# Turning the scan's output in whole 128x128 tiles, and summing log decays as two f16 products, in a hybrid attention and gated DeltaNet block

## The chip, the cores and the metric

One NeuronCore of one Trainium2 chip runs the whole kernel. The metric is device time of one execution in microseconds, the median of several runs. The five engines have queues of their own: PE (TensorE, matrix products; PEld is its weight load), DVE (VectorE), ACT (ScalarE), POOL (GpSimd) and SP (SyncE, here only an issuer of DMAs). They meet at semaphores.

## The reference, cut to what matters

A decoder block of width 1024 on 1024 tokens. One projection feeds two token mixers on the same normalised input: A, dilated sliding-window attention; B, gated DeltaNet (8 heads, key and value width 64, chunks of 64 tokens). Each is gated, projected up, and both are merged and projected out. The change touches two places of mixer B: the sums of log decays, and the way from the scan's output to the gated product.

```python
G = jnp.cumsum(gc, axis=-1)                       # log decays of a chunk
decay_incl = jnp.exp(jnp.where(causal, G[..., :, None] - G[..., None, :], -jnp.inf))
a = jnp.einsum('bhnid,bhnjd->bhnij', k_beta, kc) * decay_strict
t_inv = lax.linalg.triangular_solve(eye + a, ...)
...
o_b = _gated_delta_rule(gq, gk, gv, g, beta)
o_b = _rmsnorm(o_b, gdn_norm_w[layer]).reshape(b, s, GDN_V_WIDTH)
y_b = (o_b * jax.nn.silu(gdn_z)) @ w_up_b[layer]
```

## The kernel before

**Filler.** The big projections run as filler: `feed.tick(n)` puts n steps into PE's order, each of three f16 products of 512 columns (lines 183, 184, 185: high by high, low by high, high by low; every f32 operand of a projection is split into an f16 high part and an f16 rest). Small stages put ticks between their own steps, so that PE has work while other engines do theirs. PE's order is the order of the program, written out by hand; the order of the other engines is decided by a scheduler.

**Memory of PE's results.** PSUM is used through rings of banks of 128x512 f32, named by what they serve: mm (three buffers, the projections), G and S (two each), O (one).

**Log decays** (`in_chunks`, `decay`, lines 1110 to 1189). `gg` holds the log decays, 128 tokens (two chunks) by 8 tiles by 8 heads. Tile t holds, for the four heads of one half `hb`, a product `gm` of the decays with the triangle `upto64` on DVE, 128x256. PE multiplies `gm` by the constant triangle `later` (line 1185, f32), which gives sums of decays between every two tokens; a second product (line 1186, bf16) adds the mask; ACT takes the exponential into `E`. Two ticks follow. There are 16 such steps, 8 in each half. `gm` has two buffers, and the first two steps use a spare tile `room`, which the trace calls x.

**Triangular solve and merge** (lines 1295 to 1373). For each half `hb`, DVE inverts the 32x32 blocks in one long chain (`stmp` and `X` in turn; `As` is its input), SP writes the result out and loads it back in another layout as `T1p` and `MT`, and PE merges the blocks (`left`, line 1339, and `right`, line 1354), with DVE's `Y` between the two.

**Turning the scan's output** (lines 1731 to 1758). `ob` holds the scan's output, tokens on the partitions. Each of four channel tiles `ct` and two token halves `hf` is turned: eight f32 transposes of 64 rows (line 1745), four into a bank G and four into a bank S; DVE multiplies each bank, 256 columns, into the gate `zs[ct]` (named `zb` in the trace; two operations); ACT writes the f16 high part and DVE the f16 rest into `osb`; then two ticks. `zb`, `osb` and the low half of an output weight, `wo6l`, share a ring of five buffers, `oTb`. The eight products `ob<-ob,fac` on DVE stand just ahead, with 12 ticks behind them.

Of the kernel before, what the change touches and what calls it, by code (L numbers as in the profile page):

```python
# [10 lines left out]
F32 = mybir.dt.float32  # L11
F16 = mybir.dt.float16
BF16 = mybir.dt.bfloat16
AF = mybir.ActivationFunctionType
ALU = mybir.AluOpType
# [3 lines left out]
S = 1024  # L19
D = 1024  # L20
KT = 8
EPS = 1e-6
H_SCALE = 16.0
# [54 lines left out]
def hybrid_block(ctx: ExitStack, tc: tile.TileContext, A):  # L78
    nc = tc.nc
    V, SC, PE, GP = nc.vector, nc.scalar, nc.tensor, nc.gpsimd  # L80

    def STT(out, in0, scalar, in1, op0, op1, eng=None):
        (eng or V).scalar_tensor_tensor(out, in0, scalar, in1, op0=op0, op1=op1)  # L83

    def TT(out, in0, in1, op, eng=None):
        (eng or V).tensor_tensor(out, in0, in1, op)  # L86

    ctx.enter_context(tc.manual_schedule(engines={nc.tensor.engine}))
    base = ctx.enter_context(tc.tile_pool(name="base", bufs=1))
# [6 lines left out]
    start = [ctx.enter_context(ExitStack()) for _ in range(2)]  # L96
# [27 lines left out]
    ident = part(128)  # L124
    normw = part(KT)
    later = part(128)
# [3 lines left out]
    upto64 = part(64)  # L130
# [4 lines left out]
    gnw = part(1)  # L135
# [251 lines left out]
    feed = Feed()  # L387
# [9 lines left out]
    diag = base.tile([128, 2, 128], F32, name="diag", tag="diag", bufs=1)  # L397
# [84 lines left out]
    src = [A["w"][att_unit(2, 0, i)] for i in range(2)]  # L482
# [13 lines left out]
    with tc.manual_schedule(engines={nc.vector.engine, nc.scalar.engine}):  # L496
        wq, wk = w_first
        q, k = qk
# [63 lines left out]
        q = [bank("mm", 3), bank("O", 1)]  # L562
# [342 lines left out]

    wba = wst.tile([128, 4, 256], F32, name="wba", tag="wstage", bufs=2)[:, 0, :128].rearrange("p (k c) -> p k c", c=16)
    nc.gpsimd.dma_start(out=wba, in_=A["w_ba"])
    wbas = base.tile([128, KT, 32], F16, name="wbas", tag="diag", bufs=1)
    SC.activation(wbas[:, :, 0:16], wba, AF.Copy, scale=W_SCALE)
    STT(wbas[:, :, 16:32], wba, W_SCALE, wbas[:, :, 0:16], ALU.mult, ALU.subtract)  # L910

# [155 lines left out]
    for t in range(8):  # L1067
        tk = slice(t * 128, t * 128 + 128)
        for k in range(KT):
            PE.matmul(pba[:, t * 32:t * 32 + 32], lhsT=h_hi[:, k, tk], rhs=wbas[:, k], start=(t == 0 and k == 0),  # L1070
                      stop=False, skip_group_check=True)
            PE.matmul(pba[:, t * 32:t * 32 + 16], lhsT=h_lo[:, k, tk], rhs=wbas[:, k, 0:16], start=False,
                      stop=(k == KT - 1), skip_group_check=True)
# [5 lines left out]
    beta, gg = bg[:, 0], bg[:, 1]  # L1079
# [34 lines left out]
    def in_chunks(pg):  # L1114
        ggf = gg.rearrange("p t h -> p (t h)")
        PE.matmul(pg[:, 0:64], lhsT=upto, rhs=ggf, start=False, stop=True, skip_group_check=True)
        PE.matmul(pg[:, 64:128], lhsT=later, rhs=ggf, start=False, stop=True, skip_group_check=True)
        SC.activation(eG.rearrange("p t h -> p (t h)"), pg[:, 0:64], AF.Exp)
        by_chunk(eGs, eG)
        SC.activation(eGl.rearrange("p t h -> p (t h)"), pg[:, 64:128], AF.Exp)  # L1120
        SC.activation(dec.rearrange("p t c q -> p (t c q)"), pg[:, 128:192], AF.Exp)

    feed.later(PG_LAG, over_chunks)
    feed.tick(ATT_LEAD)
# [9 lines left out]
    p2_ = pctx.enter_context(tc.tile_pool(name="gpre2", bufs=1))  # L1134

    def bc(x, n):
        return x[..., None].to_broadcast(list(x.shape) + [n])
# [29 lines left out]
    def heads_h2(x):  # L1167
        return x.rearrange("p t (q e) -> p t e q", e=2)

    def decay(hb):  # L1170

        gh = heads_h2(gg[:, :, 4 * hb:4 * hb + 4])
        for t in range(8):
            if hb == 0 and t < 2:

                if t == 0:
                    room = wst.tile([128, 512], F32, name="x7", tag="x7", bufs=1)
                gm = room[:, 256 * t:256 * t + 256].rearrange("p (e q i) -> p e q i", e=2, q=2)
            else:
                gm = p2_.tile([128, 2, 2, 64], F32, name="gm", tag="gm", bufs=2)  # L1180
            TT(gm, bc(gh[:, t], 64), upto64[:, None, None, :].to_broadcast([128, 2, 2, 64]), ALU.mult)
            if t == 0:
                feed.tick(GM_LAG)
            p = bank("G", 2)
            PE.matmul(p[:, :256], lhsT=later, rhs=gm.rearrange("p a b c -> p (a b c)"), start=True, stop=False)
            PE.matmul(p[:, :256], lhsT=ident_b, rhs=hide_b[:, None, :].to_broadcast([128, 4, 64]),
                      start=False, stop=True)
            SC.activation(E[hb][:, t].rearrange("p a b c -> p (a b c)"), p[:, :256], AF.Exp)
            feed.tick(2)
# [269 lines left out]
    osp = {}  # L1459
    zs = {}  # L1460
    late = []
# [29 lines left out]

    def z_keep(br, ct, hf, p, rest):
        if ct not in zs:
            zs[ct] = late[1].tile([128, S], F32, name=f"zb{ct}", tag="oTb", bufs=5)
        z_silu(zs[ct][:, hf * 512:hf * 512 + 512], p, rest)

    for u in range(2):
# [159 lines left out]
    def rows(b):  # L1657
        return slice(64 * b, 64 * b + 64)
# [75 lines left out]
    for t in range(8):  # L1734
        TT(ob[:, t], ob[:, t], bc(fac[:, t], 64), ALU.mult)
    feed.tick(OB_LAG)
    for ct in range(4):
        for hf in range(2):
            ts = slice(hf * 512, hf * 512 + 512)
            ps2 = [bank("G", 2), bank("S", 2)]  # L1740
            hb, h0 = ct // 2, ct % 2 * 2
            for t in range(4):
                for b in range(2):
                    c2 = b ^ hb
                    PE.transpose(ps2[b][:, 64 * t:64 * t + 64],
                                 ob[rows(b), 4 * hf + t, 4 * c2 + h0:4 * c2 + h0 + 2].rearrange("p h v -> p (h v)"),
                                 ident[rows(b), rows(b)])
            zv = zs[ct][:, ts].rearrange("p (t c i) -> p t c i", c=2, i=64)
            for b in range(2):
                zc = zv[:, :, b ^ hb]  # L1750
                STT(zc, ps2[b][:, :256].rearrange("p (t i) -> p t i", i=64), gnw, zc, ALU.mult, ALU.mult)
            if ("b", ct) not in osp:
                osp["b", ct] = fpb.tile([128, 2, S], F16, name=f"osb{ct}", tag="oTb", bufs=5)
            n = osp["b", ct]
            sc = H_SCALE
            SC.activation(n[:, 0, ts], zs[ct][:, ts], AF.Copy, scale=sc)
            STT(n[:, 1, ts], zs[ct][:, ts], sc, n[:, 0, ts], ALU.mult, ALU.subtract)
            feed.tick(2)
    feed.until(("gate", 6))
    feed.tick(1)  # L1760
    cctx.close()
# [12 lines left out]
    for n in range(7):  # L1774
        wo7[n] = []
        for i, l in enumerate("hl"):
            if n == 5:
                t = [late[0].tile([128, 512], F32, name=f"wo5{l}{b}", tag=("gst", "oa")[i], bufs=2).bitcast(F16)
                     .rearrange("p (k n) -> p k n", n=512) for b in range(2)]
                wo7[n].append(lambda k, t=t: t[k // 2][:, k % 2])  # L1780
                continue
            if (n, l) == (6, "l"):
                t = late[1].tile([128, 2, S], F16, name="wo6l", tag="oTb", bufs=5)
                t = t.rearrange("p a b -> p (a b)").rearrange("p (k n) -> p k n", n=512)
            else:
                t = fp2.tile([128, 4, 512], F16, name=f"wo{n}{l}")
            wo7[n].append(lambda k, t=t: t[:, k])
# [2 lines left out]
    feed.flush()  # L1790

    m7.append([late[1].tile([128, 2, S], F16, name=f"mb{n}", tag=f"osa{n}" if n < 4 else "oTb",
                            bufs=1 if n < 4 else 5).rearrange("p l (k i) -> p l k i", i=256) for n in range(7)])
    fw = fp2.tile([128, D], F32, name="fw")
    nc.sync.dma_start(out=fw, in_=A["fnw"])

# [193 lines left out]
```

## Time and profile before

| | |
|---|---|
| runs of the kernel before | 1077.85, 1081.21, 1081.53 us; median 1081.21 |
| profiled execution, own time | 1077.67 us |
| its span | 1075.9 us |
| granted TensorE clock, mean | 0.998 |
| sums of log decays | 561.7 to 606.0 us (first gm to last product) |
| solve of the second half on DVE | 673.7 to 713.3 us |
| turning of the output | 889.3 to 904.4 us |

Times of the trace count from the start of the span. A row of the timeline gives start, length, engine, line, operation, what it writes and reads, the shape and a count; in brackets stands the idle time before it and who ended it. A matmul's length includes its way through the array, and the next starts before it ends, so PE's pace is the distance between starts. A row of a tile or line view gives minimum, median and maximum in ns.

### The profile page before, as it was taken

To read this page: it belongs to the slowest core of one execution; us is meant where nothing else is said; L and a number is where in the kernel's file an instruction comes from. 1 tells how busy PE (TensorE), PEld (TensorE's weight loads), DVE (VectorE), ACT (ScalarE), POOL (GpSimd) and SP (SyncE) were. 2 spreads that over 40 slices of the span, in tenths; PEclk is the share of its full clock that TensorE was granted. 3 is DMA by queue.
4 is the path that set the end of the run, shared out by engine and by line. 5 is a ranking of instruction groups with operands and counts; after the bars stand their busy time and mean duration, and the time that the engine had idled before them with its cause. 6 is when DMAs were issued, how large, how long until landed. Compare 5 with 4: busy or idle time off the path is not lost.

```text
span 1075.9 us, 23729 instructions
## 1 busy us (share of the span) xinstructions
PE 1051.3 (98%) x9430; PEld 639.9 (59%) x9430; DVE 860.6 (80%) x1977; ACT 560.1 (52%) x1272; POOL 56.9 (5%) x107
## 2 busy tenths in 40 slices
PE   7999999999999999999999999999999999999997
PEld 5995685775956855765645555555555554444443
DVE  6987997869878779979955897976588778899934
ACT  6455766566566666557634624244444345333622
POOL 0000000000000000000000001111100000000000
PEclk9999999999999999999999999999999999999999
DMA  8144531633625432741234357785685523753232
GB/s 277 62 130 106 139 104 55 168 100 88 179 70 150 110 105 63 176 114 46 75 123 162 88 130 195 244 249 164 193 268 163 160 82 121 271 195 121 78 117 79
DMA packets 99488, 148.47 MB, mean 138 GB/s; under 512 B 31136, under 2 KB 64416, under 8 KB 98224
## 3 DMA queue, kind: packets, MB, share of 16 engines
q1 hardware_dynamic: 68976, 84.60, 27.2%
q0 software_dynamic: 12320, 44.11, 13.6%
q10 hardware_dynamic: 18080, 18.23, 5.0%
q8 instruction: 74, 1.21, 0.5%
q14 instruction: 38, 0.31, 0.1%
HBM read 91.13 MB, written 36.90 MB: 119 GB/s over the span
## 4 chain that ended last, share of the span: by engine, by line
PE 68%; DVE 21%; ACT 5%; issue 2%; DMA 2%; SPq 1%; ACTq 0%; DVEq 0%
PE ps_mm L183 17%; PE ps_mm L185 16%; PE ps_mm L184 16%; DVE ca L83 3%; DVE wlo L83 2%; DVE sm L799 2%; PE ps_S L183 2%; PE ps_S L185 2%; PE ps_S L184 2%; PE ps_G L813 1%; DVE tl L86 1%; DVE rt L86 1%; SPq L629 1%; ACT sm L803 1%; PE ps_G L185 1%
## 5 line engine op out<-in xcount | busy, mean ns | idle before, releaser
L185 PE MATMUL ps_mm<-h_hi,wlo 128*128 128x512 f16 (+1 forms) x552 | 207.5, 376 | 0.0
L183 PE MATMUL ps_mm<-h_hi,whi 128*128 128x512 f16 (+1 forms) x492 | 185.0, 376 | 0.3 <-issue 0.3
L184 PE MATMUL ps_mm<-h_lo,whi 128*128 128x512 f16 (+1 forms) x492 | 184.8, 376 | 0.0
L185 PEld LDWEIGHTS <-wlo 128*128 128x128 f16 x788 | 77.1, 98 | 86.3
L183 PEld LDWEIGHTS <-whi 128*128 128x128 f16 x848 | 83.0, 98 | 70.8 <-issue 0.4
L184 PEld LDWEIGHTS <-whi 128*128 128x128 f16 x848 | 83.0, 98 | 67.3 <-issue 0.8
L183 PE MATMUL ps_mm<-whi,h_hi 128*128 128x256 f16 x384 | 105.1, 274 | 0.0
L185 PE MATMUL ps_mm<-whi,h_lo 128*128 128x256 f16 x384 | 104.7, 273 | 0.0
L184 PE MATMUL ps_mm<-wlo,h_hi 128*128 128x256 f16 x384 | 104.7, 273 | 0.0
L803 ACT ACTIVATE sm<-sm,osb 128x128 f32<-128x128 f32 (+1 forms) x160 | 69.5, 435 | 65.5 <-DVE osb L799 58.8
L86 DVE TENSOR_TENSOR tl<-ps_G,th 128x256 f16<-128x256 f32 (+1 forms) x96 | 51.9, 541 | 21.7 <-ACT th L818 21.2
L83 DVE SCALAR_TENSOR_TENSOR wlo<-wstage,whi 128x1024 f16<-128x1024 f32 x50 | 60.9, 1221 | 3.1 <-ACT whi L166 3.1
L799 DVE CUSTOM_DVE_ANT_0 sm<-ps_S,amask 128x128 f32<-128x128 f32 (+1 forms) x192 | 59.3, 347 | 4.7 <-PE ps_S L792 4.6
L83 DVE SCALAR_TENSOR_TENSOR ca<-xc,cw,ca 128x512 f32<-128x512 f32 x72 | 53.8, 747 | 7.2 <-ACT ca L1006 6.4
L166 ACT ACTIVATE whi<-wstage 128x1024 f16<-128x1024 f32 x49 | 51.3, 1052 | 2.2 <-ACT gst L944 0.8
L83 DVE SCALAR_TENSOR_TENSOR whi<-wstage,whi 128x512 f16<-128x512 f32 x60 | 40.9, 688 | 13.5 <-ACT whi L330 12.9
L813 PE MATMUL ps_G<-cons,sm 128*128 128x128 f32 x280 | 47.8, 275 | 2.8 <-ACT sm L803 1.3
L330 ACT ACTIVATE whi<-wstage 128x512 f16<-128x512 f32 x60 | 37.1, 626 | 18.6 <-DVE wstage L329 13.5
L184 PEld LDWEIGHTS <-h_hi 128*128 128x128 f16 x384 | 45.8, 119 | 1.6
L813 PEld LDWEIGHTS ps_G<-cons,sm 128*128 128x128 f32 x280 | 35.5, 141 | 18.9 <-ACT sm L803 4.6
L183 PE MATMUL ps_mm<-h_hi,wlo 128*128 128x512 f16 x120 | 45.6, 380 | 1.0 <-DVE rx L83 1.0
L183 PEld LDWEIGHTS <-h_hi 128*128 128x128 f16 x384 | 45.6, 119 | 1.5
(443 smaller groups left out, 2595.6 us busy)
## 6 DMA issues: line engine op xcount, KB each, us to landing
wstage<-in_w POOLq DMA_DIRECT2D x68, 512.0 KB, 4.9
og<-osb ACTq DMA_DIRECT2D x32, 132.0 KB, 2.3
og<-og SPq DMA_DIRECT2D x32, 132.0 KB, 2.2
gspb<-gst ACTq DMA_DIRECT2D x16, 256.0 KB, 2.5
sga<-gspa SPq DMA_DIRECT2D x8, 512.0 KB, 7.1
wstage<-in_w_up POOLq DMA_DIRECT2D x8, 512.0 KB, 5.7
wos<-in_w_out SPq DMA_DIRECT2D x8, 512.0 KB, 5.5
sgb<-gspb SPq DMA_DIRECT2D x8, 512.0 KB, 5.7
```

The lines of the kernel that those rows point to most:

```text
L83: (eng or V).scalar_tensor_tensor(out, in0, scalar, in1, op0=op0, op1=op1)
L86: (eng or V).tensor_tensor(out, in0, in1, op)
L166: in_turn(SC.activation(hi[:, 4 * c:4 * c + 4], st, AF.Copy, scale=W_SCALE))
L183: PE.matmul(out, lhsT=wh(k), rhs=mh(k), start=first and i == 0, stop=False, skip_group_check=True)
L184: PE.matmul(out, lhsT=wh(k), rhs=ml(k), start=False, stop=False, skip_group_check=True)
L185: last_pe[0] = PE.matmul(out, lhsT=wl(k), rhs=mh(k), start=False, stop=last and i == len(ks) - 1, skip_group_check=True).ins.name
L330: in_turn(SC.activation(t[:, b, 0], self.part[name], AF.Copy, scale=W_SCALE))
L629: nc.sync.dma_start(out=dst[r0:r0 + 32, hd], in_=pt[name[1]][32 * hd:32 * hd + 32, "AB".index(name[0])])
L799: V.tensor_tensor_reduce(P[:, u, :128 * nk], psc[:, u * 256:u * 256 + 128 * nk], mask, -cexp, -NEG, ALU.add, ALU.min, accum_out=osb[:, 256 ...
L803: SC.activation(P[:, u, :128 * nk], P[:, u, :128 * nk], AF.Exp, bias=osb[:, 256 + hd:257 + hd], scale=-1.0, accum_out=osb[:, 260 + hd:261 ...
L813: PE.transpose(pt[:, c:c + 128], P[:, u, i * 128:i * 128 + 128], ident)
```

## The change

**Decays.** `gg` is split once into an f16 high part and an f16 rest (`gsplit`: one copy and one subtraction of 128x32 for each half, in `in_chunks`), and the triangle `later` is copied to f16 once (`later16`). Both live in `wide`, a 128x512 f16 tile which takes the place and size of the tile of `wbas`. `gm` holds both parts, each multiplied by `upto64` in a single DVE operation of 512 columns, in f16, in the bytes of the old tile. The f32 product becomes two f16 products of 256 columns.

**Turning.** The loop runs over two channel pairs instead of four channel tiles. A step turns eight whole 128x128 tiles, four into bank G and four into bank S, all 512 columns of each, and serves the two channel tiles `ct` = h0/2 and 2 + h0/2: four operations `zb`, two of ACT and two `osb`; then four ticks. There are four steps instead of eight and 32 transposes instead of 64; the number of ticks stays 16.

**Ring.** `oTb` has six buffers instead of five, and the high half of the weight, `wo6h`, moves from a pool of its own into it.

```diff
-    wbas = base.tile([128, KT, 32], F16, name="wbas", tag="diag", bufs=1)
+    wide = base.tile([128, 512], F16, name="wide", tag="diag", bufs=1)
+    wbas = wide[:, :256].rearrange("p (k c) -> p k c", c=32)
+    later16 = wide[:, 256:384]
+    gsplit = wide[:, 384:512].rearrange("p (l t b h) -> p l t b h", l=2, t=8, b=2)
+    V.tensor_copy(later16, later)
...
+        for hb in range(2):
+            src = gg[:, :, 4 * hb:4 * hb + 4].rearrange("p t (q e) -> p t e q", e=2)
+            hi, lo = [gsplit[:, l, :, hb].rearrange("p t (e q) -> p t e q", e=2) for l in range(2)]
+            V.tensor_copy(hi, src)
+            TT(lo, src, hi, ALU.subtract)
...
-                gm = p2_.tile([128, 2, 2, 64], F32, name="gm", tag="gm", bufs=2)
-            TT(gm, bc(gh[:, t], 64), upto64[:, None, None, :].to_broadcast([128, 2, 2, 64]), ALU.mult)
+                gm = p2_.tile([128, 256], F32, name="gm", tag="gm", bufs=2)
+            gm = gm.bitcast(F16).rearrange("p (l a i) -> p l a i", l=2, i=64)
+            TT(gm, bc(gsplit[:, :, t, hb], 64), upto64[:, None, None, :].to_broadcast([128, 2, 4, 64]), ALU.mult)
...
-            PE.matmul(p[:, :256], lhsT=later, rhs=gm.rearrange("p a b c -> p (a b c)"), start=True, stop=False)
+            for l in range(2):
+                PE.matmul(p[:, :256], lhsT=later16, rhs=gm[:, l].rearrange("p a i -> p (a i)"), start=(l == 0),
+                          stop=False)
...
-    for ct in range(4):
+    for h0 in (0, 2):
         for hf in range(2):
             ts = slice(hf * 512, hf * 512 + 512)
             ps2 = [bank("G", 2), bank("S", 2)]
-            hb, h0 = ct // 2, ct % 2 * 2
             for t in range(4):
-                for b in range(2):
-                    c2 = b ^ hb
-                    PE.transpose(ps2[b][:, 64 * t:64 * t + 64],
-                                 ob[rows(b), 4 * hf + t, 4 * c2 + h0:4 * c2 + h0 + 2].rearrange("p h v -> p (h v)"),
-                                 ident[rows(b), rows(b)])
...
-            feed.tick(2)
+                for c2 in range(2):
+                    PE.transpose(ps2[c2][:, 128 * t:128 * t + 128],
+                                 ob[:, 4 * hf + t, 4 * c2 + h0:4 * c2 + h0 + 2].rearrange("p h v -> p (h v)"), ident)
+            for hb in range(2):
+                ct = 2 * hb + h0 // 2
+                zv = zs[ct][:, ts].rearrange("p (t c i) -> p t c i", c=2, i=64)
+                for c2 in range(2):
+                    zc = zv[:, :, c2]
+                    STT(zc, ps2[c2].rearrange("p (t b i) -> p t b i", b=2, i=64)[:, :, c2 ^ hb], gnw, zc,
+                        ALU.mult, ALU.mult)
...
+            feed.tick(4)
...
-            if (n, l) == (6, "l"):
-                t = late[1].tile([128, 2, S], F16, name="wo6l", tag="oTb", bufs=5)
+            if n == 6:
+                t = late[1].tile([128, 2, S], F16, name=f"wo6{l}", tag="oTb", bufs=6)
```

The order of the engines at three places, before and after. First, PE's order at one of the 16 decay steps (LDWEIGHTS is the load of the stationary operand; an f32 product has its own inside):

```order
L185 MATMUL ps_mm<-h_hi,wlo 128x512
L1185 MATMUL ps_G<-gm,cons 128x256
L1186 LDWEIGHTS ident_b
L1186 MATMUL ps_G<-hide_b,ident_b 128x256
L183 LDWEIGHTS whi
```

```order
L185 MATMUL ps_mm<-h_hi,wlo 128x512
L1195 LDWEIGHTS wide
L1195 MATMUL ps_G<-gm,wide 128x256
L1195 LDWEIGHTS wide
L1195 MATMUL ps_G<-gm,wide 128x256
L1197 LDWEIGHTS ident_b
L1197 MATMUL ps_G<-hide_b,ident_b 128x256
L183 LDWEIGHTS whi
```

The f32 product is gone and two f16 products with a weight load each stand in its place; nothing around them moves. Second, DVE's order where it begins to read the turned output (numbers behind zb and osb tell the channel tiles apart):

```order
L83 SCALAR_TENSOR_TENSOR zb_11257<-ps_G,cons,zb_11257 128x4x64
L83 SCALAR_TENSOR_TENSOR zb_11257<-ps_S,cons,zb_11257 128x4x64
L83 SCALAR_TENSOR_TENSOR wlo<-wstage,wlo 128x512
L83 SCALAR_TENSOR_TENSOR zb_11257<-ps_G,cons,zb_11257 128x4x64
L83 SCALAR_TENSOR_TENSOR osb_12044<-zb_11257,osb_12044 128x512
L83 SCALAR_TENSOR_TENSOR zb_11257<-ps_S,cons,zb_11257 128x4x64
```

```order
L83 SCALAR_TENSOR_TENSOR zb_11278<-ps_G,cons,zb_11278 128x4x64
L83 SCALAR_TENSOR_TENSOR zb_11278<-ps_S,cons,zb_11278 128x4x64
L83 SCALAR_TENSOR_TENSOR wlo<-wstage,wlo 128x512
L83 SCALAR_TENSOR_TENSOR zb_11609<-ps_G,cons,zb_11609 128x4x64
L83 SCALAR_TENSOR_TENSOR osb_12065<-zb_11278,osb_12065 128x512
L83 SCALAR_TENSOR_TENSOR zb_11609<-ps_S,cons,zb_11609 128x4x64
```

The kinds stand in the same order, but the fourth and the sixth now read the banks of the first step for a second channel tile, where before they read those of the second step. Third, DVE's order where the solve of the second half begins:

```order
L86 TENSOR_TENSOR rv<-ps_O,bg 128x512
L86 TENSOR_TENSOR As<-As,bsc 128x1024
L83 SCALAR_TENSOR_TENSOR wlo<-wstage,whi 128x1024
L86 TENSOR_TENSOR As<-As,bsc 128x1024
L86 TENSOR_TENSOR Y<-ps_S,pack 32x512 x2
L86 TENSOR_TENSOR rv<-ps_O,bg 128x512
L83 SCALAR_TENSOR_TENSOR wlo<-wstage,whi 128x1024
L86 TENSOR_TENSOR stmp<-As,X 128x31
```

```order
L86 TENSOR_TENSOR rv<-ps_O,bg 128x512
L83 SCALAR_TENSOR_TENSOR wlo<-wstage,whi 128x1024
L86 TENSOR_TENSOR Y<-ps_S,pack 32x512 x2
L86 TENSOR_TENSOR rv<-ps_O,bg 128x512
L86 TENSOR_TENSOR As<-As,bsc 128x1024
L83 SCALAR_TENSOR_TENSOR wlo<-wstage,whi 128x1024
L86 TENSOR_TENSOR As<-As,bsc 128x1024
L86 TENSOR_TENSOR stmp<-As,X 128x31
```

The two products on `As` moved behind `Y` and `rv`, which read banks that PE fills in the merge of the first half.

More of the change, by code (lines that the diff above doesn't have):

```diff
@@ L1170, in decay @@
     def decay(hb):
-        gh = heads_h2(gg[:, :, 4 * hb:4 * hb + 4])
         for t in range(8):
@@ L1177, in decay @@
                     room = wst.tile([128, 512], F32, name="x7", tag="x7", bufs=1)
-                gm = room[:, 256 * t:256 * t + 256].rearrange("p (e q i) -> p e q i", e=2, q=2)
+                gm = room[:, 256 * t:256 * t + 256]
             else:
-                gm = p2_.tile([128, 2, 2, 64], F32, name="gm", tag="gm", bufs=2)
-            TT(gm, bc(gh[:, t], 64), upto64[:, None, None, :].to_broadcast([128, 2, 2, 64]), ALU.mult)
+                gm = p2_.tile([128, 256], F32, name="gm", tag="gm", bufs=2)
+            gm = gm.bitcast(F16).rearrange("p (l a i) -> p l a i", l=2, i=64)
+            TT(gm, bc(gsplit[:, :, t, hb], 64), upto64[:, None, None, :].to_broadcast([128, 2, 4, 64]), ALU.mult)
             if t == 0:
@@ L1493, in z_keep @@
         if ct not in zs:
-            zs[ct] = late[1].tile([128, S], F32, name=f"zb{ct}", tag="oTb", bufs=5)
+            zs[ct] = late[1].tile([128, S], F32, name=f"zb{ct}", tag="oTb", bufs=6)
         z_silu(zs[ct][:, hf * 512:hf * 512 + 512], p, rest)
@@ L1740, in hybrid_block @@
             ps2 = [bank("G", 2), bank("S", 2)]
-            hb, h0 = ct // 2, ct % 2 * 2
             for t in range(4):
-                for b in range(2):
-                    c2 = b ^ hb
-                    PE.transpose(ps2[b][:, 64 * t:64 * t + 64],
-                                 ob[rows(b), 4 * hf + t, 4 * c2 + h0:4 * c2 + h0 + 2].rearrange("p h v -> p (h v)"),
-                                 ident[rows(b), rows(b)])
[L1748 to L1757, printed above, removed]
-            feed.tick(2)
+                for c2 in range(2):
[8 more added lines that the diff above has]
+                        ALU.mult, ALU.mult)
+                if ("b", ct) not in osp:
+                    osp["b", ct] = fpb.tile([128, 2, S], F16, name=f"osb{ct}", tag="oTb", bufs=6)
+                n = osp["b", ct]
+                sc = H_SCALE
+                SC.activation(n[:, 0, ts], zs[ct][:, ts], AF.Copy, scale=sc)
+                STT(n[:, 1, ts], zs[ct][:, ts], sc, n[:, 0, ts], ALU.mult, ALU.subtract)
+            feed.tick(4)
     feed.until(("gate", 6))
@@ L1792, in hybrid_block @@
     m7.append([late[1].tile([128, 2, S], F16, name=f"mb{n}", tag=f"osa{n}" if n < 4 else "oTb",
-                            bufs=1 if n < 4 else 5).rearrange("p l (k i) -> p l k i", i=256) for n in range(7)])
+                            bufs=1 if n < 4 else 6).rearrange("p l (k i) -> p l k i", i=256) for n in range(7)])
     fw = fp2.tile([128, D], F32, name="fw")
```

## The prediction

> **What bounds the kernel now.** The page comes first: span, busy shares, and the chain that ended last.
>
> ```profile
> span 1075.9 us, 23729 instructions
> PE 1051.3 (98%) x9430; PEld 639.9 (59%) x9430; DVE 860.6 (80%) x1977; ACT 560.1 (52%) x1272; POOL 56.9 (5%) x107
> PE 68%; DVE 21%; ACT 5%; issue 2%; DMA 2%; SPq 1%; ACTq 0%; DVEq 0%
> ```
>
> PE is busy for 98% of the span, so a microsecond of matmul taken off PE shortens the run wherever PE is fed all the time; DVE holds a fifth of the chain, so there are stretches where PE's order waits for it. The windows say which stretches the change meets (columns: length, then busy time and count of PE, PEld, DVE, ACT, POOL, then the granted clock, the DMA share, GB/s).
>
> ```profile
> 400.00:540.00 140.00, 135.86 (x1212) 89.85 (x1210) 127.77 (x399) 86.86 (x230) 5.28 (x10) 1.00 0.35 94
> 560.00:610.00 50.00, 50.00 (x370) 28.71 (x369) 30.34 (x56) 25.20 (x46) 3.47 (x7) 1.00 0.44 136
> 890.00:900.00 10.00, 9.03 (x63) 4.22 (x64) 9.85 (x20) 4.48 (x8) 1.05 (x2) 1.00 0.37 125
> ```
>
> The sums of log decays lie in 560 to 610: PE busy 50.00 of 50.00 us, DVE only 30.34. The turning of the scan's output lies near 890 to 905: there DVE is the full engine (9.85 of 10) and PE has holes. The small casts that the change adds fall into 400 to 540, where DVE is 91% busy and PE 97%. The list of PE's waits (us in total, times, longest) shows what those holes wait for.
>
> ```profile
> PE ps_G L813 <- DVE tl L86: 1.1, 1, 1.1
> PE ps_G L1745 <- DVE zb L83: 0.5, 1, 0.5
> ```
>
> **Part 1, sums of log decays: −3.45 us.** The timeline of PE at one of the 16 places, then a run of 256-column f16 products elsewhere.
>
> ```profile
> 563.23 0.38 PE L185 MATMUL ps_mm<-h_hi,wlo 128*128 128x512 f16 x1
> 563.45 0.59 PE L1185 MATMUL ps_G<-gm,cons 128*128 128x256 f32 x2
> 563.88 0.27 PE L1186 MATMUL ps_G<-hide_b,ident_b 128*128 128x256 bf16 x1
> ...
> 460.07 0.27 PE L183 MATMUL ps_mm<-whi,h_hi 128*128 128x256 f16 x1
> 460.18 0.27 PE L184 MATMUL ps_mm<-wlo,h_hi 128*128 128x256 f16 x1
> ```
>
> Matmuls are pipelined, so I use the distance between starts, not the length of one. The f32 product (two passes in the trace) holds PE from 563.45 to 563.88, 0.43 us. An f16 product of 256 columns holds it 0.11, 460.07 to 460.18, where the weights change with every matmul as they will here. Two of them take 0.22, so each place gives 0.43 − 0.22, more exactly 0.216 us (half of 0.43), and 16 places 3.45 us. PE has no hole in this window, so all of it is on the path. Bounds: nothing, if an f16 pass took as long as an f32 pass (0.43/2 = 0.215 each), against 3.45; the rows at 460 are the same shape and type, so I take 3.45.
>
> What this costs DVE: the operand gm grows from 256 to 512 columns.
>
> ```profile
> L86 DVE TENSOR_TENSOR gm<-bg,cons x14: 419/425/426, 561.7 to 603.2; 128x256 f32<-128x256 f32 x14
>   PE ps_G L1185: 11.2, 8
> L86 DVE TENSOR_TENSOR ob<-ob,fac x8: 684/686/693, 887.3 to 891.5; 128x512 f32<-128x512 f32 x8
> ```
>
> From 425 to about 686 ns (a 128x512 product of the same kind) is 0.26 us each, 3.7 us for the 14 tiles in this window. The second row, from the view of gm's tile, is DVE's idle time before gm: it waited 11.2 us in 8 places for PE to free the buffer, 1.4 us each, so it is early by more than the 0.26. I cost this at nothing; the cover is that idle time. Were it gone, 3.7 us would fall on PE.
>
> **Part 2, casts and longer first tiles, before 500 us: +0.5 us.**
>
> ```profile
> 476.90 0.42 DVE L1098 TENSOR_SCALAR gx<-bg,cons 128x64 f32<-128x64 f32 x2
> 477.23 0.75 DVE L86 TENSOR_TENSOR x<-bg,cons 128x256 f32<-128x256 f32 x2
> 482.74 1.22 DVE L83 SCALAR_TENSOR_TENSOR wlo<-wstage,whi 128x1024 f16<-128x1024 f32 x1 [0.47 <-ACT whi L166]
> ```
>
> Two operations of 128x32 go ahead of x here, about 0.2 us each by the gx row (64 columns), and the two x products grow by 0.26 each: 0.4 + 0.52 = 0.9 us. DVE has 0.47 us of idle before the wlo at 482.74, which absorbs half; what is left delays the tl for which PE waits 1.1 us already (list above, L813). So PE loses 0.9 − 0.47, about 0.45; the second pair (0.4 us, some 20 us later) I take to be mostly absorbed. The early cast of the triangle (128x128) meets an early stretch and is counted within the same 0.5. Bounds: 0, if later slack takes it, and 0.9 + 0.4 = 1.3, if none does. I take 0.5, nearest to the row with the idle time.
>
> **Part 3, turning the output: −2.15 us.** PE's timeline at the first of the eight blocks now, at the last, and, from another stage, at four whole f32 transposes.
>
> ```profile
> 889.00 0.38 PE L185 MATMUL ps_mm<-h_hi,whi 128*128 128x512 f16 x1
> 889.31 0.27 PE L1745 MATMUL ps_G<-cons,ob 64*128 64x64 f32 x1
> 889.31 0.27 PE L1745 MATMUL ps_S<-cons,ob 64*128 64x64 f32 x1
> ...
> 903.72 0.38 PE L185 MATMUL ps_mm<-h_hi,wlo 128*128 128x512 f16 x1
> 904.43 0.39 PE L183 MATMUL ps_mm<-sum4h,whi 128*128 128x512 f16 x1
> ...
> 574.46 0.60 PE L1220 MATMUL ps_S<-cons,kT 128*128 128x128 f32 x4
> 574.90 0.38 PE L183 MATMUL ps_mm<-h_hi,whi 128*128 128x512 f16 x1
> ```
>
> A 512-column product holds PE 0.216 us (from two rows under the rivals, 14 products apart), a filler step of three 0.649, and the stage has 16 steps before and after: 10.38 us. It begins when PE comes free at 889.00 + 0.22 = 889.22 and ends two steps after the last block, at 904.43 + 1.30 = 905.73: 16.51 us. The last block held nobody up and cost 904.43 − (903.72 + 0.22) = 0.49; eight such are 3.95. What remains, 16.51 − 10.38 − 3.95 = 2.18 us, is waiting for DVE. Changed: four whole transposes took 574.90 − 574.46 = 0.44, so a block of eight takes 0.87 and four blocks 3.48, which is 0.47 less than 3.95. How much of the waiting stays is read from the DVE rows (three lie between the two, and PE's first block stands ahead).
>
> ```profile
> 893.94 0.48 DVE L83 SCALAR_TENSOR_TENSOR zb<-ps_G,cons,zb 128x256 f32<-128x256 f32 x1
> ...
> 895.73 0.68 DVE L83 SCALAR_TENSOR_TENSOR osb<-zb,osb 128x512 f16<-128x512 f32 x1
> ```
>
> Each bank has two buffers, so the third block needs those of the first, now read by four zb instead of two. In the new order DVE does zb, zb, wlo, zb, osb, zb: the very kinds of these rows up to the osb, then a zb, which ends about 895.73 + 0.6 + 0.48 = 896.8 if DVE, full here, starts the first zb where it does now. PE gets there at 889.22 + 2 × (0.87 + 4 × 0.649) = 896.15. So it waits about 0.5, and the rest, 2.18 − 0.5 = 1.68, goes: 0.47 + 1.68 = 2.15. PE's four steps of filler between blocks cover the other zb. Bounds: −0.5, if DVE's fullness makes PE wait as long in total as now, and −2.65, without any wait.
>
> The Trainium skill, "TensorEngine Tiling (Array Packing)", Theoretical Speedup, gives up to twice the speed where a dimension is 64 or less, because row tiles work in parallel (Key Properties); that speaks against giving up the 64-row halves. The trace agrees that the halves in ps_G and ps_S start together (889.31 and 889.31).
>
> **Part 4, the ring of six buffers and wo6h: nothing.** The weight loads and casts stay the same in kind and number, and no PE wait on them stands in the list. Bounds: nothing gained, as nothing is waited for; at most the 0.5 us of the zb wait above is lost again if an early buffer keeps osb back.
>
> **The sum:** −3.45 + 0.5 − 2.15 = −5.1 us. Against the profiled execution's own time, 1077.67 us (span 1075.9, and 1.8 around it), this is 1072.6. The median of the runs shown is 1081.21, 3.5 above that execution, so the same change gives 1076.1 there, −0.47%. A measurement of this kernel can tell about 0.5% (5.4 us) from no change, so the forecast lies just inside that line.
>
> **Rivals.**
>
> *A. A wait in the merge of the second half eats the gain of part 1.* The rows: PE ahead of that merge, SP's load that it needs, this load's time to landing (min, median, max), the SP issue behind which the load of As now moves, As's own landing, and the first step of DVE's solve, from which T1p comes.
>
> ```profile
> 729.86 0.38 PE L183 MATMUL ps_mm<-h_hi,whi 128*128 128x512 f16 x1
> 732.88 0.38 PE L185 MATMUL ps_mm<-h_hi,wlo 128*128 128x512 f16 x1
> 733.19 1.20 PE L1339 MATMUL ps_S<-T1p,MT 32*32 32x32 f32 x64
> 723.15 2.30 SPq L1322 DMA_DIRECT2D T1p<-t_d x1
> DMA to landing us min/median/max: 3.2/6.6/7.4
> 666.05 0.44 SPq L1381 DMA_DIRECT2D rvt<-rv_d x1
> DMA to landing us min/median/max: 3.8/4.0/4.1
> 673.70 0.18 DVE L86 TENSOR_TENSOR stmp<-As,X 128x31 f32<-128x31 f32 x1
> ```
>
> (729.86 to 732.88 are 14 products: 0.216 each.) T1p lands near 723.15 + 6.6 = 729.75, by the longest 730.55, and PE uses it at 733.19: slack 3.4 or 2.6 us. PE will come 3.45 − 0.5 = 2.95 earlier. DVE's solve does not: in the new order the two As products stand behind Y and rv, for which PE must come first, and I reckon its first step 1.1 us earlier (672.6). SP's queue moves too: As is issued behind rvt, near 666.5 − 2.95 = 663.5, and lands 4.0 later, at 667.5, in time for that. Slack left: 3.4 − 2.95 + 1.1 = 1.5, so no wait. If T1p lands no earlier than now, PE waits 0 to 0.4 by these landings; if the solve loses 2 us more than reckoned, 2 to 2.4. Then the total is −5.1 + 2 = −3: 1078. For it: DVE's rows there follow each other without a hole. Chance 0.15.
>
> *B. DVE sets the pace of the turning*, part 3 is worth 0.5 only: −3.45 + 0.5 − 0.5 = −3.45: 1077.8. For it: 9.85 of 10 us busy. Against: the number of DVE operations does not grow, and the filler between blocks is twice as long. Chance 0.07.
>
> *C. Whole transposes cost twice the halves*: a block of eight takes 4 × 0.49 = 1.97, four blocks 7.9 instead of 3.48, +4.4: in all −0.7, 1080.5. Against: the four whole f32 transposes at 574.46 took 0.11 each. Chance 0.02. This is what the Trainium skill's factor of up to two, on the page and in the section named above, would make of it.
>
> *D. Slower.* The same merge, further: were the solve's result later by d against now, PE would wait d − 0.45 (3.4 − 2.95), and the total is −5.1 + d − 0.45. It turns positive at d = 5.6 and passes +0.5% at d = 11, about nine operations of 128x1024 on DVE at 1.22 us (the wlo row of part 2). Speaking for it: the solve is one long chain, in which DVE puts whatever is ready. Against it: from the second As product to the end of the chain, the same operations stand there in both orders. With d = 11.5: +5.9, 1087. Chance 0.07.
>
> *E. More than forecast*: no wait in the turning (−2.65) and casts that cost nothing: −6.1, 1075.1. Chance 0.07.
>
> That the change does not do what it says I leave at nothing: in the new order PE has 32 f16 products and 32 whole transposes in the places of the old ones.
>
> **How the numbers follow.** The forecast has 0.62, at −5.1 with its own spread of about −4.2 to −6: 0.33 of this past 5.4 us, 0.29 short of it. Faster: 0.33 + 0.07 (E) = 0.40. Same: 0.29 + 0.15 (A) + 0.07 (B) + 0.02 (C) = 0.53. Slower: 0.07 (D). Predicted: 1076.1. The range: the costs' own bounds give −6.1 to −0.5 around 1081.21, 1075.1 to 1080.7; the runs shown differ by 3.7 among themselves (1077.85 to 1081.53), so I extend it downwards by most of this: 1071 to 1081.5. D and the ends of the scatter lie outside.
>
> **What would show it.** Part 1: from the filler's last product to the mask's product it is 0.65 us now (563.23 to 563.88) and should be 0.44: two products 0.11 apart, PE still without a hole in that stage, and gm at 0.69 us with DVE still waiting for PE there. Part 2: PE's wait at L813 for tl grows from 1.1 to about 1.6. Part 3: four blocks of 0.87 and one wait for zb near 0.5; a sum of waits near 2 means B, blocks near 2 us mean C. A and D: a PE wait at the merge's matmul (L1339 before) for T1p. The prediction is wrong if a wait of over 2 us appears on PE that neither list names, or if the f16 products stand 0.2 apart.

## The result and the profile after

| | before | after |
|---|---|---|
| median | 1080.41 us (20 runs, 1077.47 to 1085.96) | 1076.91 us (20 runs, 1072.81 to 1079.83) |
| ratio | | 0.9969, 95% interval 0.9957 to 0.9980 |
| profiled execution, own time | 1077.67 us | 1078.95 us |
| its span | 1075.9 us | 1077.2 us |

The change makes the kernel 3.5 us faster in the median. The one profiled execution of it is among its slower ones (20 runs spread over 7 us), the one of before among the fastest of before, and so it is 1.3 us longer than that of before. That is useful: it shows where the gain can be lost. One execution of all that follow, in e6, ran at a granted clock of 0.753 and took 1361.78 us; the ratio of e6 leaves it out. The page of the changed kernel, span, busy time and chain:

```profile
span 1077.2 us, 23669 instructions
PE 1049.5 (97%) x9398; PEld 639.4 (59%) x9398; DVE 864.0 (80%) x1982; ACT 559.2 (52%) x1272; POOL 56.1 (5%) x107
PE 51%; DVE 31%; DMA 8%; ACT 4%; issue 3%; SPq 2%; DVEq 0%; ACTq 0%
```

DMA holds 8% of the chain that ended last, where it held 2% before. PE's waits in the changed kernel (us in total, times, longest), the ones that answer to those quoted of before:

```profile
PE ps_S L1350 <- DMA T1p<-t_d: 4.0, 1, 4.0
PE ps_G L813 <- DVE tl L86: 1.2, 1, 1.2
PE ps_S L1754 <- DVE zb L83: 0.5, 1, 0.5
```

The first is new: at the first product of the second half's merge, PE stands for 4.0 us until T1p has landed. PE's timeline at a decay step, at that merge, and around the turning:

```profile
562.86 0.38 PE L185 MATMUL ps_mm<-h_hi,wlo 128*128 128x512 f16 x1
563.08 0.38 PE L1195 MATMUL ps_G<-gm,wide 128*128 128x256 f16 x2
563.29 0.27 PE L1197 MATMUL ps_G<-hide_b,ident_b 128*128 128x256 bf16 x1
...
729.35 0.24 PE L1350 MATMUL ps_S<-T1p,MT 32*32 32x32 f32 x2
733.58 1.91 PE L1350 MATMUL ps_S<-T1p,MT 32*32 32x32 f32 x62 [3.99 <-DMA T1p<-t_d]
735.42 0.61 PE L183 MATMUL ps_mm<-h_hi,whi 128*128 128x512 f16 x1
736.67 0.63 PE L183 MATMUL ps_mm<-h_hi,whi 128*128 128x512 f16 x1
...
891.70 0.27 PE L1754 MATMUL ps_G<-cons,ob 128*128 128x128 f32 x1
892.63 0.38 PE L183 MATMUL ps_mm<-h_hi,whi 128*128 128x512 f16 x1
899.43 0.30 PE L1754 MATMUL ps_S<-cons,ob 128*128 128x128 f32 x1 [0.48 <-DVE zb L83]
906.28 0.38 PE L183 MATMUL ps_mm<-sum4h,whi 128*128 128x512 f16 x1
```

From the filler's product to the mask's, a decay step now takes 0.43 us (562.86 to 563.29; 0.65 before): the pair of f16 products holds PE 0.21. The turning runs from 891.70 to 906.28, 14.58 us against 16.51, with one wait of 0.48. On PE both parts do what they say. PE comes to the merge at 729.35 instead of 733.19, 3.84 us earlier, and loses all of that and more there. Behind the wait, the step of three filler products from 735.42 to 736.67 takes 1.25 us instead of 0.65: the clock has dropped. Windows of 2 us there (PE's busy time is the third number, the granted clock the third from the end):

```profile
728.00:730.00 2.00, 1.59 (x9) 0.58 (x7) 1.96 (x4) 0.72 (x2) 0.00 (x0) 1.00 1.03 206
730.00:732.00 2.00, 0.00 (x0) 0.00 (x0) 1.09 (x4) 1.67 (x3) 0.54 (x1) 1.00 1.07 257
732.00:734.00 2.00, 0.42 (x16) 0.42 (x18) 1.93 (x3) 0.00 (x0) 0.00 (x0) 0.73 1.07 319
734.00:736.00 2.00, 2.00 (x56) 1.63 (x53) 0.75 (x2) 0.72 (x2) 0.00 (x0) 0.50 1.05 365
736.00:738.00 2.00, 2.00 (x7) 0.65 (x5) 0.91 (x2) 0.00 (x0) 0.00 (x0) 0.50 0.60 185
738.00:740.00 2.00, 2.00 (x9) 1.24 (x8) 0.00 (x0) 0.00 (x0) 0.00 (x0) 0.57 0.15 27
740.00:742.00 2.00, 2.00 (x87) 1.10 (x88) 0.72 (x2) 1.76 (x3) 0.00 (x0) 1.00 0.04 8
```

After 4 us without work PE ran at half clock for about 6 us (0.50 from 734 to 738, 0.57 to 740), which costs some 3 us more by the rows above (1.25 us for a step instead of 0.65). Of the next stage, the products on rvt and MT, the first starts late:

```profile
750.13 0.34 PE L1413 MATMUL ps_G<-rvt,MT 64*64 64x64 f32 x8
```

In the kernel before, the same product:

```profile
747.64 0.34 PE L1402 MATMUL ps_G<-rvt,MT 64*64 64x64 f32 x8
```

So between 729 and 750 the changed kernel turned a lead of 3.84 us into a lag of 2.49: 6.33 us, which is the wait of 3.99 and about 2.8 at half clock, less the 0.5 that before waited for Y there. The turning then takes back 1.9.

The same windows show the last number but one, the DMA share: over 1.0 until 736. Windows of 10 us before, then after:

```profile
705.00:715.00 10.00, 10.00 (x48) 4.57 (x47) 8.22 (x19) 3.09 (x6) 3.52 (x5) 1.00 0.93 306
715.00:725.00 10.00, 10.00 (x106) 4.78 (x104) 5.66 (x10) 4.80 (x9) 0.34 (x1) 1.00 1.03 264
725.00:735.00 10.00, 10.00 (x167) 5.76 (x167) 9.00 (x14) 5.08 (x10) 2.17 (x4) 1.00 0.99 246
```

```profile
705.00:715.00 10.00, 10.00 (x48) 4.53 (x47) 9.17 (x22) 3.25 (x6) 2.55 (x4) 1.00 0.85 261
715.00:725.00 10.00, 10.00 (x165) 5.36 (x164) 6.36 (x10) 5.68 (x11) 0.56 (x1) 1.00 0.80 224
725.00:735.00 10.00, 6.01 (x79) 3.62 (x79) 8.22 (x13) 4.19 (x10) 1.62 (x3) 0.90 1.10 256
```

Before, the DMA engines are full or nearly so from 705 to 735 (0.93 to 1.03). After, they are less busy until 725 (0.85 and 0.80) and fuller behind it (1.10), in the very ten us in which T1p and MT are loaded. The loads of T1p after the change, the SP row of the last of the four and the times to landing of all four (two in each half):

```profile
722.33 3.69 SPq L1333 DMA_DIRECT2D T1p<-t_d  x1
DMA to landing us min/median/max: 5.6/9.7/11.2
```

The load is issued 0.8 us earlier than before (722.33 against 723.15) and lands some 4 us later: it took the longest of these times, 722.33 + 11.2 = 733.5, just when PE goes on; before, the same load took 6.3 us and landed at 729.4.

### The profile page after: what moved, and what is told of

It is laid out like the page before. It is cut to its first block, busy times and chain, and to the rows that moved or that the text cites. A ratio compares the mean times of both kernels' runs of the same rounds, so it can differ in the third digit from the quotient of the medians.

```text
span 1077.2 us, 23669 instructions
## 1 busy us (share of the span) xinstructions
PE 1049.5 (97%) x9398; PEld 639.4 (59%) x9398; DVE 864.0 (80%) x1982; ACT 559.2 (52%) x1272; POOL 56.1 (5%) x107
## 4 chain that ended last, share of the span: by engine, by line
PE 51%; DVE 31%; DMA 8%; ACT 4%; issue 3%; SPq 2%; DVEq 0%; ACTq 0%
PE ps_mm L183 13%; PE ps_mm L185 12%; PE ps_mm L184 12%; DVE ca L83 3%; DVE wlo L83 3%; DVE rt L86 2%; DVE X L86 2%; DVE stmp L86 2%; DVE sm L799 2%; DVE tl L86 1%; PE ps_G L813 1%; SPq L629 1%; DMA wos<-in_w_out 1%; ACT sm L803 1%; DVE rx L86 1%
## 5 line engine op out<-in xcount | busy, mean ns | idle before, releaser
L813 PE MATMUL ps_G<-cons,sm 128*128 128x128 f32 x280 | 47.9, 275 | 2.3 <-DVE tl L86 1.2
L185 PEld LDWEIGHTS <-h_lo 128*128 128x128 f16 x384 | 45.5, 119 | 1.4
```

The lines of the kernel that those rows point to most:

```text
L185: last_pe[0] = PE.matmul(out, lhsT=wl(k), rhs=mh(k), start=False, stop=last and i == len(ks) - 1, skip_group_check=True).ins.name
L813: PE.transpose(pt[:, c:c + 128], P[:, u, i * 128:i * 128 + 128], ident)
```

## The experiments

All ratios are to runs of the kernel before on the same chip in the same session. Three sets were run: e1 to e4, e5 to e8, e9 to e11. The change itself was measured in a session of its own, so e3 to e7 and e11 can be held against it only by these ratios.

| | what | runs | median us | before | ratio | 95% interval |
|---|---|---|---|---|---|---|
| | the change | 20 | 1076.91 | 1080.41 | 0.9969 | 0.9957 to 0.9980 |
| e1 | decay part alone | 12 | 1079.83 | 1079.61 | 0.9995 | 0.9982 to 1.0008 |
| e2 | turning part alone | 12 | 1077.18 | 1079.61 | 0.9976 | 0.9964 to 0.9988 |
| e3 | change, T1p loads ahead of MT | 12 | 1078.20 | 1079.61 | 0.9982 | 0.9967 to 0.9996 |
| e4 | change, merge six steps later | 12 | 1079.12 | 1079.61 | 0.9985 | 0.9969 to 1.0001 |
| e5 | change, kbt loads behind MT | 7 | 1074.81 | 1080.65 | 0.9941 | 0.9921 to 0.9962 |
| e6 | change, a_d stores behind un_d | 12 | 1074.63 | 1080.65 | 0.9951 | 0.9933 to 0.9969 |
| e7 | change, both moves | 6 | 1074.73 | 1080.65 | 0.9942 | 0.9920 to 0.9965 |
| e8 | before, both moves | 12 | 1078.95 | 1080.65 | 0.9991 | 0.9975 to 1.0007 |
| e9 | decay part alone, both moves | 10 | 1076.20 | 1079.72 | 0.9968 | 0.9954 to 0.9981 |
| e10 | turning part alone, both moves | 12 | 1078.02 | 1079.72 | 0.9985 | 0.9970 to 1.0000 |
| e11 | change, both moves, again | 5 | 1074.63 | 1079.72 | 0.9956 | 0.9939 to 0.9973 |

**First set: is it the merge, and is it T1p?** Theory M: PE arrives early at the merge and waits for T1p. Rival S: the wait in the one profile is chance, and the rest of the shortfall lies elsewhere.

e1 keeps the decay part and puts the old loop of the turning back, with the ring of five.

> The decay part of the change alone: f16 split, two f16 products, longer gm; the turning, its ticks and the ring of five stay as before. Theory M (PE reaches the merge of the second half some 3 us earlier, T1p does not land earlier, PE waits there and its clock falls behind the wait): a PE wait for T1p at the merge's first product of 2 to 4 us as in the changed kernel, granted clock below 1.00 in 730 to 740; of the 3.45 us taken off PE about 1 to 1.5 remain, so about 1079 beside 1080.4 before. Rival S (the wait in the one profile is chance; the shortfall of the whole change lies in the DVE stretch before 500 us or in the turning): no such wait, about 2.5 to 3 us faster than before, 1077.5.

The decay part alone gives nothing (0.9995), less than either theory said. Its profile has a new wait at the merge, but for another load:

```profile
PE ps_G L1365 <- DMA MT<-u_d: 2.0, 1, 2.0
```

e2 keeps the turning part and the ring of six, with the old decays.

> The turning part alone, with the ring of six: four blocks of eight whole transposes, decays as before. Theory M: PE comes to the merge as late as before, no wait of PE for T1p, and the turning gives its 2 us in full: about 1078.3 beside 1080.4. Rival S: the turning gives 0.5 to 1 us, 1079.5 to 1080.

2.6 us faster by the ratio: the turning gives its part in full. No wait for T1p came, as expected, but the merge was not free of waits: its profile, the slowest of its runs, has PE at the merge's second group waiting for MT.

```profile
PE ps_G L1354 <- issue: 2.2, 1, 2.2
PE ps_G L1354 <- DMA MT<-u_d: 1.6, 1, 1.6
```

So the loads can come late for PE even with the old decays. How often they do, with the old decays and with the new, one profile of each kernel does not show.

e3 re-orders SP's queue alone (the edit also swaps the stores of u_d and t_d in the source; in the trace SP still issues u_d first, at 712.30, and t_d at 713.36):

```diff
-        for kb in range(4):
-            b = kb % 2
-            if b == 0:
-                nc.sync.dma_start(out=T1p[32 * kb:32 * kb + 32]...)
+        for kb in (0, 2):
+            nc.sync.dma_start(out=T1p[32 * kb:32 * kb + 32]...)
+        for kb in range(4):
+            b = kb % 2
             nc.sync.dma_start(out=U[32 * kb:32 * kb + 32]...)
```

> The changed kernel with SP's queue alone re-ordered: t_d is stored as before, but both T1p loads go ahead of the MT loads that stood between them; PE, DVE, ACT and POOL keep their order. Theory M: the second T1p load no longer waits behind an MT load (2.99 us of issue in the profile of the changed kernel), lands 3 to 4 us earlier, the wait of 4.0 us at the merge falls to 0 to 1, the clock stays at 1.00 there, and the time falls by 2 to 4 us against the changed kernel: 1073 to 1075. Rival S: no change, 1077.

The wait for T1p fell to 0.5 us as M said, and the time did not: PE now waits for MT.

```profile
PE ps_G L1365 <- DMA MT<-u_d: 3.4, 1, 3.4
PE ps_S L1350 <- DMA T1p<-t_d: 0.5, 1, 0.5
```

SP's queue in that run shows why: the three MT loads of 128 KB behind T1p keep it busy for 10.63 us, and the last of them lands near 739.6, no earlier than in the changed kernel (739.9). One MT load still stands ahead of T1p.

```profile
719.88 1.50 SPq L1331 DMA_DIRECT2D T1p<-t_d  x2
721.43 10.63 SPq L1335 DMA_DIRECT2D MT<-u_d  x3
```

e4 moves filler from behind the merge to ahead of it:

```diff
-STATE_LAG = 6
+STATE_LAG = 12
-Q_LAG = (14, 4)
+Q_LAG = (14, 0)
-UW_LAG = (12, (10, 4), 6)
+UW_LAG = (12, (10, 2), 6)
```

> The changed kernel with six filler steps (3.9 us of PE work) moved from behind the merge of the second half to ahead of it; the total number of steps is the same. Theory M: T1p has landed or all but landed when PE comes, wait 0 to 1 us, clock 1.00, and 2 to 4 us faster than the changed kernel, 1073 to 1075, unless the steps taken away behind the merge uncover a new wait there. Rival S: no change, 1077.

No PE wait for T1p or MT is left, but the caveat came true: without the steps behind the merge PE waits 3.0 us for ACT in the products that follow (764.38), so this run does not tell M from S by its time.

```profile
PE ps_S L1266 <- ACT uw L1424: 3.0, 1, 3.0
```

M as it stood (T1p alone) falls with e3. What e1 to e4 have in common is that something loaded or made late meets PE there. Theory D took its place: the DMA engines are full ahead of the merge (the windows above), and PE's earlier arrival moves none of the bytes that lie ahead of T1p and MT. Rival L: the chain of solve, store and load is merely long, whatever else is moved.

**Second set: lighten the queue ahead of T1p and MT.** Two moves, both only of DMA issues; PE, DVE and ACT keep their order. e5: the two kbt loads of the second half (512 KB each, needed after the merge) were issued by SP ahead of or between these loads, and go behind them.

```diff
+            if kb == 3:
+                mt_dma[hb] = mt.ins.name
...
-            nc.sync.dma_start(out=kb, in_=kb_d[hb][:, ts])
+            kbi = nc.sync.dma_start(out=kb, in_=kb_d[hb][:, ts])
+            if hb:
+                tc.add_manual_dep(kbi.ins, mt_dma[1], order_only, reason="kbt behind MT")
```

> The changed kernel; in SP's queue the two kbt loads of the second half (512 KB each) go behind the T1p and MT loads; PE, DVE, ACT and POOL keep their orders. Theory D (the stretch 705 to 738 us is full with DMA, the last T1p or MT load lands near 738 to 740 however early PE comes, so PE's gain from the decays is given back at the merge): T1p and MT are issued and land 1 to 3 us earlier, PE's wait at the merge for them, 4.0 in the profile of the changed kernel, falls to 1 to 2, and the time by 1 to 2.5 us: 1075. Rival L (not the DMA traffic but the chain solve, store, load alone sets the landing; its length is latency): landings stay, no change, 1077.

e6: the stores of the first half's a_d (512 KB each, read again only by the scan) go behind the un_d stores of the second half.

```diff
         pairs(hb, qT, E[hb])
-        spill(hb)
+        if hb:
+            spill(hb)
...
             state_side(1)
+            spill(0)
```

> The changed kernel; on POOL's queue the two a_d stores of the first half (512 KB each, issued at 727 and 731 us in the profile of the changed kernel) go behind the un_d stores of the second half, past the merge; the other engines keep their orders. Theory D: a tenth of the stretch's bytes leaves it, but the last part, so only the last two MT loads land earlier, by 1 to 3 us: 0.5 to 2 us faster, 1075 to 1076.5. Rival L: no change, 1077.

e7 has both, and e8 has both in the kernel before.

> Both: kbt loads behind MT on SP, a_d stores behind un_d on POOL. Theory D: the last MT load lands near 734 to 736, no PE wait over 1 us at the merge, the clock stays at 1.00 in 728 to 745, 2 to 4 us faster than the changed kernel: 1073 to 1075. Rival L: no change, 1077.

> The kernel before (f32 decay product, half transposes) with both of these moves. Theory D: here PE comes 3 us later, so the moves help only those executions in which MT came late: 0 to 2 us faster than before, 1078 to 1080; and with the merge free in both, the change is worth its full 4.5 to 5.5 us between this kernel and the one with both moves. Rival P (PE time saved in the decays is not worth its 3.45 us for a reason other than the merge): the two differ by 2 to 3 us only, as the turning alone gave.

Each move brings the changed kernel to 0.994 to 0.995, and together they bring no more. Each of these intervals overlaps that of the change (0.9957 to 0.9980), so no single one of them proves a gain over it; e5, e6, e7 and e11 all lie below it. L falls: the landings move, and further than expected. In e7 SP issues all six loads within 5 us, and T1p lands sooner than in the changed kernel (median 4.8 us against 9.7). The last MT load lands at 728.5 in e5 and 726.6 in e7, against 739.9, though the solve's own store landed no earlier (t_d at 720.0 and 719.0, against 717.5).

```profile
717.56 0.32 SPq L1337 DMA_DIRECT2D MT<-u_d  x1
718.98 0.32 SPq L1335 DMA_DIRECT2D T1p<-t_d  x1
719.35 0.57 SPq L1337 DMA_DIRECT2D MT<-u_d  x1
719.97 0.60 SPq L1335 DMA_DIRECT2D T1p<-t_d  x1
720.61 1.86 SPq L1337 DMA_DIRECT2D MT<-u_d  x2
```

```profile
DMA to landing us min/median/max: 3.2/4.8/9.2
```

Between 700 and 800 us the longest PE wait in e7 is one of 0.5 us for DVE's Y:

```profile
PE ps_G L1369 <- DVE Y L86: 0.9, 2, 0.5
```

e5 and e6 are less clean: e5 waits 1.1 us for Y, and e6 still 1.0 us for T1p, with the last MT load at 736.1. So for e6 the case rests on its times alone.

The kernel before gains nothing that can be told from the same moves (0.9991). So the moves are worth something because PE now comes early: with the merge free, the change takes the kernel from 0.9991 to 0.9942, 0.49% or 5.3 us (4.2 by the medians; 3.8 by the ratio of the repeat, e11), where it gave 3.5 as it stands. The forecast of the sum was 5.1.

**Third set: the parts apart, with the merge free.**

> The decay part alone with both moves (kbt behind MT, a_d behind un_d), old turning. Theory D: with the merge's loads early the decay part gives its 3.45 us less about 0.5 on DVE before 500 us: about 3 us faster than the kernel before with both moves (1078.95 beside 1080.65 before), so a ratio to before of 0.995 to 0.997, where the decay part without the moves gave 0.9995. Rival P: the decay part is worth nothing for another reason: 0.998 to 1.000.

> The turning part alone with both moves, old decays. Both theories: about 2 us faster than the kernel before with both moves, ratio to before 0.996 to 0.9985.

> The whole change with both moves once more, on the chip of the two others. If the parts add once the merge is free, its ratio to before is that of the two parts together, 0.994 to 0.995; no PE wait over 1 us between 728 and 745.

The decay part, worth nothing by itself (0.9995 in e1), is worth 0.9968 here, of which the moves alone give 0.9991: about 2.5 us are its own. The intervals of e1 and e9 do not overlap; those of e8 and e9 do by a little (0.9975 to 0.9981), so the size is less sharp than the sign. Its gain went to the merge. Even in e9 that is not wholly free: PE waits 1.1 and 0.5 us for Y there, and the clock falls to 0.50 from 738 to 740. Rival P falls. e11 repeats e7 (0.9956 and 0.9942), just above the 0.994 to 0.995 that was expected, and is near the product of the parts, 0.9968 × 0.9985 = 0.9953; its longest wait at the merge is 0.8 us for Y. e10 is less clear: 0.9985 is only 0.0006 below e8, while the turning alone gave 0.9976, and e11 and e7, which add it to e9, lie 0.0012 and 0.0026 below that. These intervals overlap, and e10's own runs still spread from 1075.37 to 1080.65. By times the turning is worth between 0.6 and 2.8 us. The traces are sharper: from its first transpose to its last the stage takes 11.88 us in all seven profiles with the new loop and 14.97 to 14.98 in all four with the old one (before, e1, e8, e9), so the turning gives its 1.93 us in e10 as well. What e10's profile loses, it loses at the merge again: 1.8 us before the last product of a group (L1358) that the records put down to no engine, then half clock to 744. From the merge's first product to the first transpose it takes 160.2 us, e8 156.2. What makes that wait is open.

The fastest version that was run is the change with either move: 1074.6 to 1074.8 us.

## Why the prediction was right or wrong

- **The number.** 1076.1 was forecast and 1076.91 measured, against 1080.41 before: −3.5 us instead of −5.1, within 0.5% as forecast and inside the range. That the number is near owes something to luck: the median of before that was shown, 1081.21, is 0.8 above that of 20 runs, and from 1080.41 the same sum gives 1075.3. Measured in the traces as below, the parts add up to −3.41 + 1.00 − 1.93 = −4.34, so about half of the shortfall of 1.6 lies in the sum itself, and the other half is left for the merge, in the median. The change's own interval, −2.2 to −4.6 us, cannot tell −4.34 from −3.5; that the merge takes something is shown by e1 beside e9. By mechanism it was rival A (−3, chance 0.15) that came, beside a part 2 twice as large as forecast.
- **Part 1, −3.45: right, 3.41 measured.** From the first product of the first step to the mask's product of the last it is 46.47 us before (559.77 to 606.24) and 43.05 after (559.83 to 602.88), and the same in every other profile without and with the decay part. DVE took the longer gm (0.686 us as reckoned) and still waited for PE there, 6.9 us in 5 places (11.2 in 8 before):

```profile
L86 DVE TENSOR_TENSOR gm<-wide,cons x14: 684/686/693, 561.7 to 600.5; 128x512 f16<-128x512 f16 x14
  PE ps_G L1195: 6.9, 5
```

- **Part 2, +0.5: wrong, 1.00 measured.** The price was right (gx to wlo takes 0.98 us more), the cover was not. The second pair of casts was absorbed, as taken. DVE's idle time of 0.47 before the second wlo, which was to absorb half, is there after the change as before: it is a wait for ACT's whi, which stands behind ACT's sm, and that waits for DVE (osbs). What delays DVE delays this too. DVE's and ACT's rows, before, then after, and the first decay product in each:

```profile
480.88 0.40 ACT L803 ACTIVATE sm<-sm,osbs 128x128 f32<-128x128 f32 x1 [0.55 <-DVE osbs L799]
559.77 0.59 PE L1185 MATMUL ps_G<-x,cons 128*128 128x256 f32 x2
```

```profile
475.95 0.42 DVE L1102 TENSOR_SCALAR gx<-bg,cons 128x64 f32<-128x64 f32 x2
480.91 0.40 ACT L803 ACTIVATE sm<-sm,osbs 128x128 f32<-128x128 f32 x1 [1.53 <-DVE osbs L799]
482.77 1.23 DVE L83 SCALAR_TENSOR_TENSOR wlo<-wstage,whi 128x1024 f16<-128x1024 f32 x1 [0.47 <-ACT whi L166]
559.83 0.38 PE L1195 MATMUL ps_G<-x,wide 128*128 128x256 f16 x2
```

Counted from gx, the last row ahead of the casts, the first decay product comes 82.88 us later before (476.90 to 559.77) and 83.88 after. The four profiles without the decay part give 82.86 to 82.88, the nine with it 83.87 to 83.90. That PE is only 0.06 late at 559.8 is chance: in this execution gx stands 0.95 sooner, and over all profiles it lies anywhere from 475.8 to 476.9, with the decay part or without. The sign that the prediction named, the wait at L813, is no measure of this: it grew from 1.10 to 1.22, but it is 0.3 to 1.1 in the profiles without the decay part.
- **Part 3, −2.15: right, 1.93 measured** (14.58 against 16.51). The first block took 0.93 (891.70 to 892.63), the second and the fourth 0.87 as forecast, and the third 1.55, of which 0.48 is the wait for zb, where 0.5 was forecast, in bank S as the new DVE order had it. B and C are refuted by these rows: the wait is 0.5 and not 2, and a whole transpose takes about 0.11 us.
- **Part 4, nothing: right** as far as the list of PE's waits shows, which has none for these weights.
- **Rival A: this is the step that failed.** The prediction put T1p's landing at issue plus 6.6 us, the median of before, and moved only the issue; that left a slack of 1.5 us. The issue did move about as reckoned (0.8 us against 1.1), but by chance: counted from gx, the solve's first step and the store of t_d come less than 0.1 us sooner than before, so the 1.1 in the slack was not there. And the time to landing, 6.3 us for this load before, was 11.2. It was no constant of the transfer: it was measured in a stretch in which DMA is full, and the weight loads and stores that PE's progress sets off move forward with PE into the same stretch (two weight loads from 727.02 and 729.03 to 723.93 and 725.94, the first a_d store from 730.23 to 727.14), while the solve that T1p waits for does not. The prediction read the DMA share of no window there. A's price also lacked a term: the half clock behind the wait, about 2.8 us.
- **D, slower through the same merge:** in the median it did not come, but in the profiled execution the merge took back 6.3 us, more than the 5.1 at which D turns slower, and that execution is 1.3 us longer than the one of before, which is among the fastest of before.

## What to carry to other kernels

Before counting time saved on a saturated engine, follow it to the next meeting with a DMA and read the DMA share of the window ahead of that meeting: here, with a share of 0.8 to 1.1, the landing did not come earlier with the issue but 4 us later. A wait that moves from one load to the next when one is pulled forward (e3) points to a full queue and not to a wrong order; try to take bytes out that are needed later, as e5 and e6 do. Before an idle time is counted as cover, follow what it waits for: if that waits in turn for the engine that is being delayed, it covers nothing. A part that gives nothing alone may be worth its full price once the next bound is eased: test it with that bound removed before it is dropped.

## What the runs showed of the hardware

A wait can cost more than its length: 4.0 us without PE work were followed by about 6 us at a granted clock of 0.50. In the decay part alone a wait of 2.0 us was followed by a clock of 1.00. This fits the Trainium skill, "TensorE: Matmul & The Clock Gate", The HAM clock gate, which puts the idle window at about 3.4 us. But e5 got the half clock, for about 3 us, after two waits of 1.15 and 0.48 us among the merge's 32x32 products, with PE busy for 2.4 of 4 us:

```profile
734.00:736.00 2.00, 1.42 (x8) 0.53 (x6) 1.90 (x4) 0.17 (x1) 0.00 (x0) 1.00 1.03 424
736.00:738.00 2.00, 0.96 (x79) 0.85 (x83) 1.90 (x3) 2.00 (x5) 0.00 (x0) 0.96 0.77 311
738.00:740.00 2.00, 2.00 (x67) 1.17 (x58) 1.77 (x3) 1.19 (x3) 0.00 (x0) 0.50 0.01 4
```

e9 shows the same after waits of 1.13 and 0.48 us, and e2 and e10 fell to 0.50 after 1.65 and 2.19 and after 0.48 and 1.85, again among the 32x32 products; e11, with 0.75 and 0.48, stayed at 1.00. So several shorter waits can do it too; whether the small products or the waits count for that was not tried.

A DMA issue can hold its queue: three loads of 128 KB, in rows of 32 f32 by the kernel's text, held SP's queue for 10.63 us in e3, and two of them for 1.86 us in e7.
